# A first modulation quarter in two halves, and nine projection groups begun over three channel quarters

## The chip, the cores and the metric

The kernel runs on one core of a Trainium2 chip. The metric is the device time of one execution in microseconds (us); lower is better. Three runs of the kernel before took 2329.36 to 2330.72 us, median 2330.3.

## What is computed

Two streams of 128 tokens with 2048 channels (context and latent) go through two layers. Each layer begins like this, and the rest follows from the column blocks of one wide projection:

```python
def trunk_layer(x, mod, l, p, lower_bounds, hg_s0, s5_s0_re, s5_s0_im, ctx_k, ctx_v, rope):
    bsz, seq, _ = x.shape
    shift, scale, gate = jnp.split(mod, 3, axis=-1)
    h = rms_norm(x, p['norm_w'][l]) * (1 + scale[:, None, :]) + shift[:, None, :]
    (hg_q, hg_i, hg_ff, hg_fb, hg_g, at_q, at_k, at_v, at_g,
     s5_u, s5_g, merge_raw) = split_columns(h @ p['w_in'][l])
```

`mod` is `silu(c) @ w_mod[l] + b_mod[l]`, one vector of 3 x 2048 per stream. The blocks feed an HGRN2 recurrence, grouped-query attention and an S5 state-space scan; the three results are merged by gates, projected (w_out), gated and added to x.

## The kernel before, in words

**Layout.** Both streams are worked on together. h lies transposed, channels on partitions: 16 k-tiles of 128 channels. A channel quarter is four k-tiles (512 channels). h is kept as a rounded part (hh) and a rest (hl), each in a tile of tag H8 for two quarters; H8 has four buffers.

**Projections.** `gemm` (line 160) takes w_in in pieces of 512 KB (two k-tiles by 512 columns), three buffers of them. ScalarE rounds a k-tile of weights (wh, line 138), VectorE subtracts (wl, line 139), and TensorE adds three products for each stream: 12 matmuls of 512 columns a piece (lines 178 to 180). wh and wl have four buffers each. `in_group` does this for one group of 512 columns, named u 0, aq 0, aq 1, akv 0, q 0, ff 0, fb 0, i 0, u 1 and so on (`GROUPS`).

**Modulation.** `mod_part` (line 245) makes one quarter of shift and scale (512 channels of each) from eight weight tiles of 1 MB; each tile is 16 matmuls of 256 columns with 32 columns of c as stationary operand, four column strips side by side (line 274). A bias transfer on POOL, an add, two transposes, two copies and one more operation end it. `normed` (line 311) then scales x (xn), transposes it and applies shift and scale: stream 0 on VectorE (line 328), stream 1 on ScalarE (line 330), then splits into hh and hl.

**The opening of layer 0.** `build` issues c and x (two transfers of 1 MB) on ACT's queue; `square` and `token_rstd` make the norm's factor. Part 0 of the modulation runs first, with buffers that are free so early (`PTAGS`). In `layer`, nine groups (the first eight of `GROUPS` and q 1) are then begun: their sums over quarter 0 are copied from PSUM to their places by ScalarE (`begin`, line 344), and their sums over quarter 1 are added there by VectorE (line 342). Meanwhile a side generator issues modulation parts 1 to 3; `side_work` takes `SRATE` = 0.67 of a weight tile from it for every piece. After that quarters 2 and 3 of h are made, and `group` (line 365) completes each begun group with eight k-tiles and one more add.

**What follows.** u 0 goes to `s5_half`, whose `s5_quarter` (line 785) prepares a quarter in the tiles Bl, S16 (Sb), CC and scans it in 64 steps of four VectorE operations (lines 828 to 834). There are four such quarters in a layer, one after another, since these tiles have one buffer each. aq and akv go to attention, q, ff, fb, i to the HGRN2 units (`hgrn_unit`), each level of which waits for the one before. `s5_finish` (line 1034) splits the S5 result into ghl and multiplies it by w_glu.

**Order of the work.** The program's order on each engine and queue is planned ahead of the run by a priority per instruction: `with self.prio(base)` gives base plus a running number, and of what is ready the lowest number goes first. P_MIX is 0, P_SCAN 500,000, P_LAST 900,000, P_TOP 1,000,000 (weights, their splitting, evacuation), P_CHAIN 2,000,000, P_S5 3,000,000, P_PREP 5,000,000 and P_PE (projection matmuls) 6,000,000. On the chip each engine runs its list in that order. Weight transfers go through SP's queue.

The functions with the lines of the profile:

Of the kernel before, what the change touches and what calls it, by code (L numbers as in the profile page):

```python
# [20 lines left out]
D = 2048  # L21
T = 128
L = 2
# [3 lines left out]
NP = T // 2  # L27
RAW = 3
MB = 2
PTAGS = [(t, 2) for t in ("Bl", "S16", "ys")] + [(("k4", "k4"), 1)] + [("H8", 2)] * 4  # L30
STAGS = (("H8", 2),)
HF = ((1, 1, 1, 1), (0, 0, 0, 0))
SRATE = 0.67
MTAGS = ((("k4", "q4"), 1), (("k4", "q4"), 1), (("k4", "k4"), 1))
MRATE = (0.36, 0.13)
MAGIC = 1.5 * 2.0 ** 23
# [25 lines left out]
class Builder:  # L62
    def __init__(self, tc, ctx, io):
        self.tc, self.nc, self.io = tc, tc.nc, io
        self.seq = 0
        pool = lambda name, bufs, **kw: ctx.enter_context(tc.tile_pool(name=name, bufs=bufs, **kw))
        self.cp = pool("const", 1)
        self.wp = pool("weights", 4)
        self.sb = pool("sb", 1)
        self.bufs = dict(H8=4, Z8=2, Bl=1, CC=1, S16=1, uT=1, U2=1, ys=1, q4=2, kv=2,  # L70
                         mo=1, st=10, k2=6, k4=3, gt=4, sm=18, s5i=4, p=4, sb=1, sc=1, s5t=1)
        self.pg = pool("pg", 4, space=PSUM)
        self.pm = pool("pm", 2, space=PSUM)
        self.pb = pool("pb", 2, space=PSUM)
        self.dr = pool("scratch", 1, space=DRAM)
        self.uid = 0
# [122 lines left out]

    def condition(self):  # L200
        nc = self.nc
        c = self.const("c", (128, 80))[:, 0:32]
        nc.scalar.dma_start(c, self.io["cT"])
        self.cT = self.const("cs", (128, 64))
        nc.gpsimd.memset(self.cT, 0.0)
        sg = self.t2("sg", (128, 32))
        nc.scalar.activation(sg, c, AF.Sigmoid)
        nc.vector.tensor_mul(self.cT[:, 0:32], c, sg)
# [36 lines left out]
    def mod_part(self, l, part, prio, tags, plan):  # L245
# [3 lines left out]

        nc, io = self.nc, self.io  # L250
        with self.prio(prio):
            bm = self.t("mo", "bm", (128, 352))[:, 0:256]
            src = io["b_mod"][l, part]
            nc.gpsimd.dma_start(bm, bass.AP(src.tensor, src.offset, [[256, 4], [0, 32], [1, 256]]))
        kb = 0
# [41 lines left out]
                self.mods[part] = mt  # L297
        yield True


    def square(self, ssq, x, s, n):
        junk = self.tg("junk")
# [2 lines left out]
    def token_rstd(self, ssq):  # L305
        tot = self.ts("tot", (128, 2))
        self.nc.vector.tensor_reduce(tot, ssq, AX.X, ALU.add)
        r = self.rstd(tot, 2, D)
        return [r[:, s:s + 1] for s in range(2)]

    def normed(self, x, rs, q):

# [28 lines left out]
        with self.prio(P_TOP):  # L341
            self.nc.vector.tensor_add(dst, dst, ps)

    def begin(self, l, name, idx, q):

        ps = self.in_group(l, name, idx, 4 * q, 4 * q + 4)
        if q == 0:
            self.begun[name, idx] = self.places(name, idx)
        for dst, p in zip(self.begun[name, idx], ps):
            if q == 0:  # L350
                self.evac(p, dst)
            else:
                self.add(dst, p)
# [11 lines left out]
    def group(self, l, name, idx, func=None):  # L365
        dst = self.begun.pop((name, idx), None)
        if dst is None:
            ps = self.in_group(l, name, idx)
            dst = self.places(name, idx)
            for s in range(2):  # L370
                self.evac(ps[s], dst[s], func)
            return dst
        ps = self.in_group(l, name, idx, 8, 16)
        for s in range(2):
            self.add(dst[s], ps[s])
            if func is not None:
                with self.prio(P_TOP):
                    self.nc.scalar.activation(dst[s], dst[s], func)
        return dst
# [262 lines left out]
    def s5_params(self, l):  # L642
# [3 lines left out]
        nc, io = self.nc, self.io  # L646
        tt, ts = nc.vector.tensor_tensor, nc.vector.tensor_scalar
        par = self.t2("par", (128, 3, 64))
        nc.scalar.dma_start(par, io["s5_par"][l])
        ar, ai, ld = (par[:, i] for i in range(3))  # L650
        wks, cnt = [], [0]

# [206 lines left out]

    def layer(self, l, x, rs):  # L860
        nc, io = self.nc, self.io
        with self.prio(P_CHAIN):
            self.normed(x, rs, 0)
        if l == 0:
            def parts():
                for p in range(1, 4):
                    yield from self.mod_part(0, p, P_CHAIN, itertools.cycle(STAGS), [("b", 8, 1)])

            self.start_side(parts(), SRATE)
            for q in range(2):  # L870
                if q == 1:
                    while 1 not in self.mods:
                        next(self.side)
                    with self.prio(P_CHAIN):
                        self.normed(x, rs, 1)
                for name, idx in GROUPS[:8] + [("q", 1)]:
                    self.begin(l, name, idx, q)
            self.finish_side()
        with self.prio(P_CHAIN):
            for q in range(2 if l == 0 else 1, 4):  # L880
                self.normed(x, rs, q)
        with self.prio(P_PREP):
            bc = lambda src: bass.AP(src.tensor, src.offset + l * 128, [[0, 128], [1, 128]])
# [188 lines left out]
    def build(self):  # L1072
        nc, io = self.nc, self.io
        self.side = None
        self.s5p, self.s5sc, self.begun, self.mods = {}, {}, {}, {}
        with self.prio(P_CHAIN):
            self.condition()
            x = [self.t8("x") for _ in range(2)]
            for s in range(2):
                nc.scalar.dma_start(x[s], io["x"][s])  # L1080
            self.ident = self.const("ident", (128, 128), src=io["ident"])
            self.normw = self.const("normw", (128, L, 16), src=io["norm_w"])
        with self.prio(P_LAST):
            ssq = self.ts("ssq", (128, 2, 4))
            for s in range(2):
                for n in range(4):
                    self.square(ssq, x, s, n)
            rs = self.token_rstd(ssq)
        for _ in self.mod_part(0, 0, P_CHAIN, iter(PTAGS), [("g", 8, 1)]):
            pass  # L1090
        with self.prio(P_PREP):
            self.setup()
            for l in range(L):
                self.s5_params(l)
        for l in range(L):
            x, rs = self.layer(l, x, rs)
            if l + 1 < L:
                def gates():
                    tags = itertools.cycle(MTAGS)
                    for p in (4, 5):  # L1100
                        yield from self.mod_part(L - 1, p, P_PE, tags, [("m", MB, MB)] * (8 // MB))

                self.gates = gates()
        with self.prio(P_TOP):
            self.final(x, rs)
# [9 lines left out]
def _mod_parts(w):  # L1115

    h = D // 4
    return np.concatenate([w[..., o + q * h:o + q * h + h] for q in range(4) for o in (0, D)] + [w[..., 2 * D:]], axis=-1)


def _layouts(a):
# [4 lines left out]
    out["norm_w"] = ca(a["norm_w"].reshape(L, 16, 128).transpose(2, 0, 1))  # L1126
    out["w_mod"] = ca(_mod_parts(a["w_mod"]).reshape(L, 8, 2, 128, 6, 1024).transpose(0, 4, 1, 3, 2, 5).reshape(L, 6, 8, 128, 2048))
    out["b_mod"] = _mod_parts(a["b_mod"]).reshape(L, 6, 1024)
    w_in = np.empty((L, len(GROUPS), 8, 128, 1024), np.float32)
    for l in range(L):  # L1130
        for gi, (n, h) in enumerate(GROUPS):
# [77 lines left out]
```

## Time and profile before

| | us |
|---|---|
| median of three runs | 2330.3 |
| the profiled execution | 2331.88 |
| its span, first to last instruction | 2330.1 |
| TensorE busy | 2257.9 |
| VectorE busy | 1798.2 |
| ScalarE busy | 1180.8 |

The span lies within the profiled execution, whose time also holds 1.8 us around it. Busy time of TensorE (PE) holds overlap of pipelined matmuls. DVE is VectorE, ACT ScalarE, POOL GpSimd, SP the queue engine; a q behind a name means its instruction queue, and PEld is the loading of stationary operands. A row of the timeline gives start, length, engine, line, operation, output<-input, shapes and count, and in brackets the idle time before it with what ended it.

### The profile page before, as it was taken

The page shows a single profiled execution, that of the slowest core. Times are in us where ns is not written, and L with a number is a line of the kernel's source. Part 1 is how long each engine was busy: PE and PEld are TensorE (multiplying, and loading weights), DVE is VectorE, ACT ScalarE, POOL GpSimd, SP SyncE. Part 2 cuts the span into 40 slices and gives each one's busy share as a digit, 9 for nine tenths or more (in the row PEclk, how much of TensorE's full clock was granted, in tenths as well). Part 3 has the DMA queues.
Part 4 walks back from the last instruction along what each step waited for, and adds up shares of the span by engine and source line. Part 5 has one row for each costly group of instructions (what it writes and reads, how often), then busy time and mean ns, then how long its engine had stood idle before and what let it go on. Part 6 is the DMA issues. An engine that isn't in the chain of part 4 may idle for free.

```text
span 2330.1 us, 38207 instructions
## 1 busy us (share of the span) xinstructions
PE 2257.9 (97%) x13192; PEld 1812.2 (78%) x13192; DVE 1798.2 (77%) x4835; ACT 1180.8 (51%) x2061; POOL 133.9 (6%) x244
## 2 busy tenths in 40 slices
PE   4999999999999999999998999999999999999997
PEld 2777877888887776887777888888878877887886
DVE  5856899799879868865565798899959968956555
ACT  3536645555554343544446565555564544454454
POOL 2000000100000100000010001000010010000000
PEclk9999999999999999999999999999999999999999
DMA  8994554355557878677874554454545677656765
GB/s 313 342 341 142 165 172 137 110 162 184 178 165 258 295 267 298 220 251 265 305 231 138 163 174 153 132 160 155 188 155 190 194 245 240 198 179 219 240 202 181
DMA packets 131490, 483.85 MB, mean 208 GB/s; under 512 B 17200, under 2 KB 17808, under 8 KB 126944
## 3 DMA queue, kind: packets, MB, share of 16 engines
q1 hardware_dynamic: 120528, 454.09, 58.2%
q0 software_dynamic: 9472, 23.97, 3.3%
q10 hardware_dynamic: 1296, 3.36, 0.4%
q8 instruction: 103, 1.69, 0.3%
q14 instruction: 91, 0.75, 0.1%
HBM read 474.36 MB, written 6.98 MB: 207 GB/s over the span
## 4 chain that ended last, share of the span: by engine, by line
PE 82%; DVE 8%; DMA 7%; issue 2%; ACT 1%; SPq 0%; POOL 0%; DVEq 0%; ACTq 0%; POOLq 0%
PE g L178 23%; PE g L180 23%; PE g L179 22%; DMA raw<-w_in 3%; DVE wl L139 3%; PE mod L274 3%; PE bu L816 3%; PE lv L432 2%; DMA raw<-w_br 2%; DMA wm<-w_mod 2%; PE tr L134 2%; PE yp L847 1%; DVE p L830 1%; DVE Sb L834 1%; ACT wh L138 1%
## 5 line engine op out<-in xcount | busy, mean ns | idle before, releaser
L138 ACT CAST wh<-raw 128x512 fp32r<-128x512 f32 x1344 | 819.4, 622 | 925.0 <-PE g L179 459.8
L139 DVE TENSOR_TENSOR wl<-raw,wh 128x512 fp32r<-128x512 f32 x1344 | 915.5, 689 | 368.5 <-ACT wh L138 319.1
L178 PE MATMUL g<-wh,hl 128*128 128x512 f32 x1984 | 785.1, 396 | 6.4 <-ACT wh L138 2.7
L179 PE MATMUL g<-wh,hh 128*128 128x512 f32 x1984 | 777.9, 392 | 0.0
L180 PE MATMUL g<-wl,hh 128*128 128x512 f32 x1984 | 700.9, 398 | 0.4 <-DVE wl L139 0.3
L178 PEld LDWEIGHTS g<-wh,hl 128*128 128x128 f32 x1984 | 373.5, 188 | 99.4 <-ACT wh L138 8.2
L179 PEld LDWEIGHTS g<-wh,hh 128*128 128x128 f32 x1984 | 373.6, 188 | 75.7 <-issue 0.2
L180 PEld LDWEIGHTS g<-wl,hh 128*128 128x128 f32 x1984 | 366.6, 189 | 82.5 <-DVE wl L139 5.8
L178 PE MATMUL g<-wh,ol 128*128 128x512 f32 x384 | 152.0, 396 | 2.5 <-ACT wh L138 2.3
L828 DVE TENSOR_TENSOR p<-s5sc,Sb 128x64 f32<-128x64 f32 x512 | 140.8, 275 | 14.9 <-ACT Sb L820 5.9
L179 PE MATMUL g<-wh,oh 128*128 128x512 f32 x384 | 149.9, 390 | 0.0
L834 DVE TENSOR_TENSOR Sb<-Sb,p 128x64 f32<-128x64 f32 x512 | 141.7, 277 | 8.9
L830 DVE TENSOR_TENSOR p<-s5sc,Sb 128x64 f32<-128x64 f32 x512 | 139.2, 272 | 0.0
L180 PE MATMUL g<-wl,oh 128*128 128x512 f32 x384 | 132.0, 393 | 0.8 <-DVE wl L139 0.8
L274 PE MATMUL mod<-wm,cs 128*32 128x256 f32 x1536 | 104.5, 404 | 26.6 <-DMA wm<-w_mod 20.1
L833 DVE TENSOR_TENSOR p<-p,p 128x64 f32<-128x64 f32 x512 | 113.6, 222 | 6.1
L274 PEld LDWEIGHTS mod<-wm,cs 128*32 128x32 f32 x1536 | 44.7, 113 | 77.1 <-DMA wm<-w_mod 24.1
L179 PE MATMUL g<-wh,mt 128*128 128x512 f32 x256 | 99.8, 390 | 0.0
L178 PE MATMUL g<-wh,mt 128*128 128x512 f32 x256 | 99.7, 389 | 0.0
L178 PEld LDWEIGHTS g<-wh,ol 128*128 128x128 f32 x384 | 72.1, 188 | 20.3 <-ACT wh L138 4.6
L180 PEld LDWEIGHTS g<-wl,oh 128*128 128x128 f32 x384 | 71.5, 188 | 17.6 <-DVE wl L139 2.4
L180 PE MATMUL g<-wl,mt 128*128 128x512 f32 x256 | 83.5, 393 | 1.7 <-DVE wl L139 1.7
(315 smaller groups left out, 2116.8 us busy)
## 6 DMA issues: line engine op xcount, KB each, us to landing
raw<-w_in SPq DMA_DIRECT2D x496, 512.0 KB, 3.8
wm<-w_mod SPq DMA_DIRECT2D x130, 512.0 KB, 7.2
raw<-w_br SPq DMA_DIRECT2D x96, 512.0 KB, 4.2
raw<-w_out SPq DMA_DIRECT2D x64, 512.0 KB, 4.3
wm<-w_mod SPq DMA_DIRECT2D x31, 1024.0 KB, 7.4
raw<-w_glu SPq DMA_DIRECT2D x16, 512.0 KB, 3.9
gb<-gate_d POOLq DMA_DIRECT2D x16, 256.0 KB, 6.0
x<-x ACTq DMA_DIRECT2D x2, 1024.0 KB, 14.0
```

Of the source, the lines that this page charges most:

```text
L134: nc.tensor.transpose(ps[:, k], src[:, k * 128:(k + 1) * 128], self.ident)
L138: self.nc.scalar.copy(hi, src)
L139: self.nc.vector.tensor_sub(lo, src, hi.bitcast(F32))
L178: nc.tensor.matmul(ps[s], lo(k)[:, sl], wh, start=(k == 0), stop=False)
L179: nc.tensor.matmul(ps[s], hi(k)[:, sl], wh, start=False, stop=False)
L180: nc.tensor.matmul(ps[s], hi(k)[:, sl], wl, start=False, stop=(k == nk - 1))
L274: nc.tensor.matmul(ps[32 * i:32 * i + 32, 0:256], self.cT[:, 2 * k:2 * k + 32], ws[k - 2 * k0][:, i * 256:i * 256 + 256], start=(k0 == kb ...
L816: nc.tensor.matmul(pps[x][:, j2, k], Bl[pr, d, ri, k, j2, :], U2[pr, j2, 2 * qh + k].rearrange("p s t -> p (s t)"), start=True, stop=True, ...
L828: tt(p0.rearrange("p d (j s) -> p d j s", s=2), view(sc, qd * 32, [[16, 2], [1, 16], [0, 2]]), view(Sb, i, [[ds, 2], [2 * W, 16], [W, 2]]) ...
L830: tt(p1, view(sc, 128 + qd * 64, [[32, 2], [16, 2], [1, 16]]), view(Sb, i + RI, [[ds, 2], [-RI, 2], [W, 16]]), ALU.mult)
L833: tt(p0, p0, p1, ALU.add)
L834: tt(cur, cur, p0, ALU.add)
```

## The change

The first modulation quarter of layer 0 (part 0) is computed in two halves of 256 channels, each from four tiles of 1 MB in a new layout (32 matmuls of 128 columns a tile); `mod_half(0)` stands before the layer, `mod_half(1)` is the first work of the side generator. x is issued on SP's queue instead of ACT's, at the same priority. `first_turned` transposes the first quarter of x times the factor before the modulation is there and leaves it in PSUM (both buffers of bank b); `normed_half` applies a half to it. The nine groups are begun in four steps, over k-tiles 0 to 2, 2 to 4, 4 to 8 and 8 to 12, each step with its own rate of side work, and `group` completes them with the last four k-tiles. The S5 parameters, computed in `build` before, are issued within the side work, their two transfers on SP at P_TOP. Part 3 of the modulation takes its buffers from Bl, S16 and ys. Two tiles lose padding and the small tag gets two more buffers.

```diff
-PTAGS = [(t, 2) for t in ("Bl", "S16", "ys")] + [(("k4", "k4"), 1)] + [("H8", 2)] * 4
-STAGS = (("H8", 2),)
+HTAGS = (("Bl", "S16", "ys", "H8"), ("H8", "H8", "Bl", "S16"))
+STAGS = (None, (("H8", 2),), (("H8", 2),), (("Bl", 2), ("S16", 2), ("ys", 2)))
-SRATE = 0.67
+SRATE = (0.45, 0.8, 0.5, 0.5)
...
-                         mo=1, st=10, k2=6, k4=3, gt=4, sm=18, s5i=4, p=4, sb=1, sc=1, s5t=1)
+                         mo=1, st=10, k2=6, k4=3, gt=4, sm=20, s5i=4, p=4, sb=1, sc=1, s5t=1)
...
-        c = self.const("c", (128, 80))[:, 0:32]
+        c = self.const("c", (128, 64))[:, 0:32]
...
-            bm = self.t("mo", "bm", (128, 352))[:, 0:256]
+            bm = self.t("mo", "bm", (128, 256))
...
+    def mod_half(self, h):
+        nc, io = self.nc, self.io
+        with self.prio(P_CHAIN):
+            bm = self.t("mo", "bm", (128, 256))[:, 0:128]
+            src = io["b_mod0"][h]
+            nc.gpsimd.dma_start(bm, bass.AP(src.tensor, src.offset, [[128, 4], [0, 32], [1, 128]]))
+            ps = self.pg.tile([128, 512], F32, tag="g", name=self.nm("mod"))
+        for i4, tag in enumerate(HTAGS[h]):
+            with self.prio(P_TOP):
+                w = self.t(tag, "wm", (128, 2048))
+                nc.sync.dma_start(w, io["w_mod0"][h, i4])
+            with self.prio(P_CHAIN):
+                for c in range(4):
+                    k = 4 * i4 + c
+                    for i in range(4):
+                        nc.tensor.matmul(ps[32 * i:32 * i + 32, 0:128], self.cT[:, 2 * k:2 * k + 32],
+                                         w[:, c * 512 + i * 128:c * 512 + i * 128 + 128], start=(k == 0),
+                                         stop=(k == 15), tile_position=(0, 32 * i))
+            if i4 < 3:
+                yield True
+        with self.prio(P_LAST):
+            nc.vector.tensor_add(bm, bm, ps[:, 0:128])
+            tr = self.transpose4(bm, 1)
+            mt = self.cp.tile([128, 2, 2, 2], F32, tag=f"modH{h}", name=self.nm("modT"))
+            nc.vector.tensor_copy(view(mt, 0, [[4, 2], [2, 2], [1, 2]]), view(tr, 0, [[64, 2], [1, 2], [32, 2]]))
+            nc.vector.scalar_tensor_tensor(mt[:, 1], mt[:, 1], 1.0, view(self.normw, 2 * h, [[0, 2], [1, 2]]),
+                                           ALU.add, ALU.mult)
+            self.halves[h] = mt
+        yield True
...
+    def first_turned(self, x, rs):
+        self.turned = []
+        for s in range(2):
+            xn = self.tg("xn")
+            self.nc.vector.tensor_scalar(xn, x[s][:, 0:512], rs[s], None, ALU.mult)
+            self.turned.append(self.transpose4(xn, ps=self.psb("tr")))
+        self.hh = [self.t("H8", "hh", (128, 8, 256), F32R)]
+        self.hl = [self.t("H8", "hl", (128, 8, 256), F32R)]
+
+    def normed_half(self, h):
...
+            hf = self.tg("hf", (128, 2, 128))
+            for j in range(2):
+                scale, shift, ps = mt[:, 1, s, j:j + 1], mt[:, 0, s, j:j + 1], self.turned[s][:, 2 * h + j]
...
+            sl = (slice(None), slice(2 * h, 2 * h + 2), slice(s * 128, s * 128 + 128))
+            self.split_from(hf, self.hh[0][sl], self.hl[0][sl])
...
-        ps = self.in_group(l, name, idx, 8, 16)
+        ps = self.in_group(l, name, idx, 12, 16)
...
-        nc.scalar.dma_start(par, io["s5_par"][l])
+        with self.prio(P_TOP):
+            nc.sync.dma_start(par, io["s5_par"][l])
...
             def parts():
+                yield from self.mod_half(1)
                 for p in range(1, 4):
-                    yield from self.mod_part(0, p, P_CHAIN, itertools.cycle(STAGS), [("b", 8, 1)])
...
+                    if p < 3:
+                        with self.prio(P_PREP):
+                            self.s5_params(p - 1)
+                    yield from self.mod_part(0, p, P_CHAIN, itertools.cycle(STAGS[p]), [("b", 8, 1)])
+
+            with self.prio(P_LAST):
+                self.normed_half(0)
+            self.start_side(parts(), 0)
+            for i, (k0, k1) in enumerate(((0, 2), (2, 4), (4, 8), (8, 12))):
+                if i == 1:
+                    while 1 not in self.halves:
+                        next(self.side)
+                    with self.prio(P_LAST):
+                        self.normed_half(1)
+                self.side_rate = SRATE[i]
+                if i > 1:
+                    while i - 1 not in self.mods:
                         next(self.side)
                     with self.prio(P_CHAIN):
-                        self.normed(x, rs, 1)
+                        self.normed(x, rs, i - 1)
                 for name, idx in GROUPS[:8] + [("q", 1)]:
-                    self.begin(l, name, idx, q)
+                    self.begin(l, name, idx, k0, k1)
             self.finish_side()
...
             for s in range(2):
-                nc.scalar.dma_start(x[s], io["x"][s])
+                nc.sync.dma_start(x[s], io["x"][s])
...
-        for _ in self.mod_part(0, 0, P_CHAIN, iter(PTAGS), [("g", 8, 1)]):
+            self.first_turned(x, rs)
+        for _ in self.mod_half(0):
             pass
         with self.prio(P_PREP):
             self.setup()
-            for l in range(L):
-                self.s5_params(l)
```

## Rows read from the trace of the kernel before

**Rows 1.** The page: the chain that ended last, share of the span by engine.

```profile
PE 82%; DVE 8%; DMA 7%; issue 2%; ACT 1%; SPq 0%; POOL 0%; DVEq 0%; ACTq 0%; POOLq 0%
```

**Rows 2.** Windows of 20 us: length, busy us of each engine, clock, DMA share, GB/s.

```profile
0.00:20.00 20.00, 5.24 (x48) 1.79 (x48) 0.19 (x1) 2.52 (x5) 7.75 (x19) 1.00 0.92 345
...
60.00:80.00 20.00, 20.00 (x132) 13.79 (x131) 18.05 (x99) 9.38 (x17) 0.00 (x0) 1.00 0.94 350
```

**Rows 3.** Timeline of the opening, all engines: start, us, engine, line, operation.

```profile
0.74 18.38 SPq L265 DMA_DIRECT2D wm<-w_mod  x9
1.18 0.94 ACTq L1080 DMA_DIRECT2D x<-x  x2
...
3.20 0.55 POOL L793 DMA_DIRECT2D C<-s_c  x1
...
5.27 0.53 POOL L121 DMA_DIRECT2D eye<-eye  x1
...
18.99 0.63 ACT L303 ACTIVATE junk<-x 128x512 f32<-128x512 f32 x1 [12.91 <-DMA wm<-w_mod]
...
26.54 0.49 DVE L322 TENSOR_SCALAR xn<-x,r 128x512 f32<-128x512 f32 x1
...
36.00 1.86 PE L274 MATMUL mod<-wm,cs 128*32 128x256 f32 x16 [0.50 <-DMA wm<-w_mod]
...
44.29 1.38 DVE L328 TENSOR_SCALAR hf<-tr,modT 128x128 f32<-128x128 f32 x4
```

**Rows 4.** Timeline of PE, 46 to 64 us, where the gemms begin.

```profile
47.62 0.79 PE L178 MATMUL g<-wh,hl 128*128 128x512 f32 x1 [0.32 <-DVE hl L139]
...
51.72 0.40 PE L179 MATMUL g<-wh,hh 128*128 128x512 f32 x1
51.95 0.40 PE L180 MATMUL g<-wl,hh 128*128 128x512 f32 x1
52.28 1.07 PE L274 MATMUL mod<-wm,cs 128*32 128x256 f32 x16
53.28 0.50 PE L178 MATMUL g<-wh,hl 128*128 128x512 f32 x1
```

**Rows 5.** A window of 2 us: PE's granted clock is the figure behind POOL.

```profile
42.00:44.00 2.00, 0.00 (x0) 0.00 (x0) 2.00 (x14) 0.00 (x0) 0.00 (x0) 0.50 0.72 259
```

**Rows 6.** Timeline of PE about the end of the second quarter.

```profile
176.93 0.39 PE L180 MATMUL g<-wl,hh 128*128 128x512 f32 x1
177.91 1.07 PE L274 MATMUL mod<-wm,cs 128*32 128x256 f32 x16 [0.60 <-DMA wm<-w_mod]
...
183.24 0.50 PE L178 MATMUL g<-wh,hl 128*128 128x512 f32 x1 [0.26 <-DVE hl L139]
```

**Rows 7.** Groups by line, 47 to 178 us.

```profile
L139 DVE TENSOR_TENSOR wl<-raw,wh 128x512 fp32r<-128x512 f32 x72 | 49.4, 692 | 30.0 <-ACT wh L138 21.7 <-PE g L180 4.5 <-PE g L179 3.8
```

**Rows 8.** Timeline of VectorE: the last add of u 0, the first scan step.

```profile
196.55 0.68 DVE L342 TENSOR_TENSOR u<-u,g 128x512 f32<-128x512 f32 x1
...
239.94 0.27 DVE L828 TENSOR_TENSOR p<-s5sc,Sb 128x64 f32<-128x64 f32 x1 [2.10 <-ACT Sb L820]
```

**Rows 9.** Line 834, the scan's last operation: length of stretch, busy us (count).

```profile
240.00:394.00 154.00, 17.71 (x64) 1.00 0.52 163
394.00:462.00 68.00, 0.00 (x0) 1.00 0.34 106
...
626.00:677.00 51.00, 0.00 (x0) 1.00 0.44 139
...
850.00:964.00 114.00, 17.70 (x64) 1.00 0.84 287
```

**Rows 10.** VectorE and PE where layer 0's S5 result enters its gemm.

```profile
977.07 0.68 DVE L139 TENSOR_TENSOR ghl<-ys,ghl 128x512 fp32r<-128x512 f32 x1
...
992.34 0.39 PE L178 MATMUL g<-wh,ghl 128*128 128x512 f32 x1
```

**Rows 11.** Timeline of PE, 383 to 394 us.

```profile
390.43 0.50 PE L178 MATMUL g<-wh,hl 128*128 128x512 f32 x1 [1.50 <-ACT ff L386]
```

More of the change, by code (lines that the diff above doesn't have):

```diff
@@ L309, in token_rstd @@
         return [r[:, s:s + 1] for s in range(2)]
+    def first_turned(self, x, rs):
[7 more added lines that the diff above has]
+    def normed_half(self, h):
+        nc = self.nc
+        mt = self.halves[h]
+        for s in range(2):
+            hf = self.tg("hf", (128, 2, 128))
+            for j in range(2):
+                scale, shift, ps = mt[:, 1, s, j:j + 1], mt[:, 0, s, j:j + 1], self.turned[s][:, 2 * h + j]
+                if HF[s][j]:
+                    nc.vector.tensor_scalar(hf[:, j], ps, scale, shift, ALU.mult, ALU.add)
+                else:
+                    nc.scalar.activation(hf[:, j], ps, AF.Identity, scale=scale, bias=shift)
+            sl = (slice(None), slice(2 * h, 2 * h + 2), slice(s * 128, s * 128 + 128))
+            self.split_from(hf, self.hh[0][sl], self.hl[0][sl])
     def normed(self, x, rs, q):
@@ L342, in add, with begin @@
             self.nc.vector.tensor_add(dst, dst, ps)
-    def begin(self, l, name, idx, q):
-        ps = self.in_group(l, name, idx, 4 * q, 4 * q + 4)
-        if q == 0:
+    def begin(self, l, name, idx, k0, k1):
+        ps = self.in_group(l, name, idx, k0, k1)
+        if k0 == 0:
             self.begun[name, idx] = self.places(name, idx)
         for dst, p in zip(self.begun[name, idx], ps):
-            if q == 0:
+            if k0 == 0:
                 self.evac(p, dst)
@@ L861, in layer @@
         nc, io = self.nc, self.io
-        with self.prio(P_CHAIN):
-            self.normed(x, rs, 0)
         if l == 0:
             def parts():
+                yield from self.mod_half(1)
                 for p in range(1, 4):
-                    yield from self.mod_part(0, p, P_CHAIN, itertools.cycle(STAGS), [("b", 8, 1)])
[L869 to L872, printed above, removed]
+                    if p < 3:
[14 more added lines that the diff above has]
+                    while i - 1 not in self.mods:
                         next(self.side)
                     with self.prio(P_CHAIN):
-                        self.normed(x, rs, 1)
+                        self.normed(x, rs, i - 1)
                 for name, idx in GROUPS[:8] + [("q", 1)]:
-                    self.begin(l, name, idx, q)
+                    self.begin(l, name, idx, k0, k1)
             self.finish_side()
         with self.prio(P_CHAIN):
-            for q in range(2 if l == 0 else 1, 4):
+            for q in range(3 if l == 0 else 0, 4):
                 self.normed(x, rs, q)
@@ L1074, in build @@
         self.side = None
-        self.s5p, self.s5sc, self.begun, self.mods = {}, {}, {}, {}
+        self.s5p, self.s5sc, self.begun, self.mods, self.halves = {}, {}, {}, {}, {}
         with self.prio(P_CHAIN):
@@ L1128, in _layouts @@
     out["b_mod"] = _mod_parts(a["b_mod"]).reshape(L, 6, 1024)
+    cols = [np.r_[256 * h:256 * h + 256, D + 256 * h:D + 256 * h + 256] for h in range(2)]
+    out["w_mod0"] = np.stack([a["w_mod"][0][:, c].reshape(4, 4, 128, 512).transpose(0, 2, 1, 3).reshape(4, 128, 2048)
+                              for c in cols])
+    out["b_mod0"] = np.stack([a["b_mod"][0][c] for c in cols])
     w_in = np.empty((L, len(GROUPS), 8, 128, 1024), np.float32)
```

## Prediction

> **What bounds the kernel now.** The chain that ended last is read first: 82% of it is TensorE [rows 1]. So time is to be had where TensorE stands idle, and the windows show where: in the first 20 us it is busy for 5.24, from 60 us on for all of a window [rows 2]. In the opening the DMA share is 0.92 at 345 GB/s: weights of the first modulation quarter are awaited. The timeline gives the steps [rows 3]: SP issues nine transfers for that quarter, ACT the two of x, the last modulation matmuls start at 36.00, the modulated h is made from 44.29, and the first projection matmul starts at 47.62 [rows 4]. A second hole comes after the second quarter: the last matmul starts at 176.93 and lasts 0.23, the next projection starts at 183.24 [rows 6], 6.1 us later, because the last modulation tile arrives last. Beside TensorE runs a second chain, the S5 scan on VectorE. Its first step is at 239.94, after u 0 was complete at 196.55 + 0.68 [rows 8]; four quarters of 64 steps follow each other [rows 9], and the result meets TensorE at 992.34 [rows 10].
>
> **The change part by part.** The sum is made against the profiled execution, 2331.88 us (span 2330.1 and 1.8 around it); the median of the runs is 1.6 lower.
>
> *Start of the projections.* Ahead of the first matmul now stand 4 MB of modulation weights for 8. What decides is x. It leaves ACT's queue, where its two issues were free beside SP's nine [rows 3], and joins SP's. Transfers with a lower priority number are issued first: on POOL, C (P_S5, 3 million) went out at 3.20 ahead of eye (P_PREP, 5 million) at 5.27, although the code calls for eye first [rows 3]. x keeps P_CHAIN, 2 million; weights and w_in pieces have P_TOP, 1 million. So I put x behind what is free to go: the half's four tiles (4 MB), three w_in pieces in their three buffers (1.5 MB), the first tile of the second half in the spare H8 buffer (1 MB) and the two par transfers (0.2 MB), which also moved to this queue. Before, 8 MB of weights and 2 MB of x had come by 36.00: 3.6 us per MB, small loads included. With x itself that makes 8.7 MB, 31.3 us. Then four squares of 0.63 (2.5); from squares to xn it took 26.54 - 18.99 = 7.55 for eight, so 2.5 besides the squares; xn 0.49, its transposes 0.6 (an estimate, about three matmuls of 0.23); half of the 1.38 of hf (0.7); half of the 1.95 from the end of hf (45.67) to 47.62 (1.0) [rows 3, 4]; 1 for hops between engines. Sum 40.1, **gain 7.5**. The half itself is ready by then.
>
> The Trainium skill, "DMA: Bandwidth & Descriptors", Queues, rings and completion order, says that each DMA engine takes turns between the queues but consumes one ring's descriptors in order. The rows agree in that x landed in time for squares at 18.99 amid nine weight tiles. By that rule a move from ACT's ring to SP's takes x's share away unless x is issued first.
>
> *Second half.* Its four tiles hold 32 matmuls of 128 columns each, where a tile of before holds 16 of 256 columns. Sixteen of those cost 1.00 between projections (52.28 to 53.28) [rows 4] and 1.86 in the opening [rows 3]. Bounds per tile: 1.0 if columns count, 2.0 if instructions do, 3.7 at the opening's pace; I take 1.5, since the interleaved row is the nearest. Two of the four tiles should pass before 40 us while TensorE waits anyway, so two lie in its way: **loss 3.0**. Were that cover gone, 6.
>
> The Trainium skill, "TensorEngine Tiling (Array Packing)", Key Properties, says that changing the tiling mode drains TensorE, which speaks against slipping more 32-column work between projections. Rows agree in kind: the matmul ahead of the group holds 0.33 instead of 0.23 (51.95 to 52.28), already near the 1.00 that I use. Four more visits at 0.2 would be 0.8 by that rule, inside my bounds.
>
> *A third quarter begun early.* It moves 18 pieces of 12 matmuls forward; at 0.23 each (51.72 to 51.95 [rows 4]) a piece is 2.7 us and 18 are 49, the same work as before, later. What it buys is that modulation parts 1 to 3 (24 MB) spread over 54 pieces (27 MB) instead of 36, so TensorE, not DMA, ends the stage, and the last part is ready four pieces ahead. Of the hole of 6.1 [rows 6] the modulation tile's 1.0 and about 0.5 of transposes stay: **gain 4.6**. The rate of the second step (0.8 in nine pieces) leaves part 1's eighth tile to the boundary; its chain is between the 4.5 worked out under the rivals and the 9.8 from 37.86 to 47.62 [rows 3, 4], and up to four halves of pieces already cast (5.4) lie in front of it: **loss 1.0**, from 0 to 4.
>
> *VectorE and PSUM.* 36 more adds of 0.68 [rows 8] are 24.5 us. In the first stage VectorE was busy 18.05 of 20 [rows 2], but part of that is S5 parameter work of lowest priority. In the nine-piece step two subtractions of 0.69 [rows 7] and two adds make 2.7 us per piece, beside TensorE's 2.7 plus 0.8 tiles of modulation: it fits, so 0, with up to 5 if it doesn't. The transposes of both streams hold both buffers of bank b until the second half is applied; part 1's accumulation waits behind that, and SP's later H8 tiles behind part 1. This costs nothing while projections feed TensorE; else it is the 1.0 above. On SP a tile of the second half waits until matmuls release its buffer, with w_in pieces queued behind it; up to 40 us nothing consumes pieces, so 0 there, and inside the 1.0 later. The bias transfer is one more POOL issue, off the path.
>
> *S5.* Parameters are computed later in VectorE's gaps: 0; were the gaps missing, their lowest priority makes them wait until the first scan needs them. Part 3 now sits in Bl and S16, so the first scan's preparation waits for its end. Padding: no instruction; 0, unsigned.
>
> Clock: where TensorE had waited, the granted clock was 0.50, the 1.2 GHz level [rows 5], and the first matmuls of before ran at it. It will again; no difference.
>
> Sum: 7.5 - 3.0 + 4.6 - 1.0 = 8.1. 2331.9 - 8.1 - 1.6 = **2322 us**. Own range 2316 to 2330, by 4 us of x's landing and the bounds above. About 0.2%, 4.7 us, is what a measurement of this kernel can tell from no change.
>
> **Rivals.**
> *x goes first.* If x is issued ahead of the weights, only 6 MB (21.6 us) precede the half's last matmuls (to 24.5); add, transpose, copies, hf and split without parameter work between them take 4.5 by the same rows: first projection at 29. Gain 18.6, all four tiles now in the way (-6), DMA tighter at the boundaries (-2), +4.6: 15.2, so **2315**. For it: both x transfers stand first in the code. Against: POOL's order.
>
> *S5 takes over (slower).* Projections from 40, the 129.5 us that two quarters took (47.62 to 177.16), 49 for the third, 4 as above: 222.6; u 0's last two pieces end at 228, and the 43.4 us from its add to the scan [rows 8] make 271.4, **31.5 us later** than 239.94. Slack: the last split of the S5 result ends at 977.75 and TensorE takes it at 992.34 [rows 10], 14.6; between the first scans lie 68 us, between the next 51 [rows 9], 17. Together 31.6: past a start of 271 the scan sets the layer's end. If Bl and S16 come free late and preparation (about 9 us, estimated) is not hidden, it starts at 280: **2339**. Against: the first scan took 154 us, the last 114 [rows 9], since attention shares VectorE; a later start shares less of it.
>
> *Handed back.* At 390.43 TensorE waited 1.50 for ScalarE to empty ff's PSUM [rows 11], which waits for the HGRN levels. If these do not come earlier, what was won earlier ends here: **2330**.
>
> **How the numbers follow.** Forecast 0.45 (0.38 beyond 0.2%, 0.07 within), x first 0.32, handed back 0.10, S5 slower 0.13. Faster 0.70, same 0.17, slower 0.13. The range reaches from the rival x first with its tiles at column pace (2311) to the beginning of the slower case (2334).
>
> **What would show it.** x's squares at 26 to 34 us and the first projection near 40 (right), below 32 (x first); the hole at the quarter's end under 2 us; per-tile cost of the half 1 to 2 us; first scan step 260 to 272 and the S5 gemm before 988. Wrong: a first projection after 45, a scan past 275, or TensorE idle for over 6 us more between 340 and 460.

## The result and the profile after

The changed kernel takes 2353.1 us (median of four runs, 2345.3 to 2354.8) against 2330.5: ratio 1.0091, 95% interval 1.0068 to 1.0113, so **slower by 0.9%**. Run again beside the experiments it took 2351.5, ratio 1.0090 (1.0077 to 1.0103). The profiled execution is the fastest of its four runs: 2345.29, span 2343.4. The two profiles so differ by 13.3 us in span; the medians differ by 19 to 23.

The page's chain, share of the span by engine, which answers to [rows 1]:

```profile
PE 87%; DVE 4%; DMA 3%; ACT 1%; issue 1%; SPq 0%; DVEq 0%; ACTq 0%
```

It shows less waiting for DMA and VectorE than before, on a longer span; it doesn't tell where the loss is. The opening answers to [rows 3]; timeline of all engines:

```profile
0.74 2.16 SPq L311 DMA_DIRECT2D wm<-w_mod  x4
...
2.94 1.54 SPq L168 DMA_DIRECT2D raw<-w_in  x3
...
6.12 0.86 SPq L1147 DMA_DIRECT2D x<-x  x2
...
9.29 3.71 SPq L311 DMA_DIRECT2D wm<-w_mod  x2
...
26.48 0.63 ACT L334 ACTIVATE junk<-x 128x512 f32<-128x512 f32 x1 [3.63 <-DMA x<-x]
...
29.59 0.63 ACT L334 ACTIVATE junk<-x 128x512 f32<-128x512 f32 x1 [0.55 <-DMA x<-x]
...
38.06 0.80 PE L178 MATMUL g<-wh,hl 128*128 128x512 f32 x1 [0.86 <-DVE hl L139]
```

x goes out behind the four tiles and three pieces and ahead of the second half's first tiles, its squares begin 7.5 us later than before, and the first projection still starts 9.6 us earlier than 47.62 [rows 4]. The second half between projections, timeline of PE:

```profile
45.74 0.39 PE L180 MATMUL g<-wl,hh 128*128 128x512 f32 x1
46.06 1.08 PE L316 MATMUL mod<-wm,cs 128*32 128x128 f32 x32
47.07 0.50 PE L178 MATMUL g<-wh,hl 128*128 128x512 f32 x1
...
51.38 2.83 PE L316 MATMUL mod<-wm,cs 128*32 128x128 f32 x96
54.13 0.50 PE L178 MATMUL g<-wh,hl 128*128 128x512 f32 x1
```

A tile of 32 matmuls takes 1.01 from start to next start, three take 2.75: as long as tiles of 16 matmuls with twice the columns. All four tiles of the second half stand here, behind the first projection. Further on, timeline of PE where TensorE stands still:

```profile
110.42 0.66 PE L134 MATMUL tr<-ident,xn 128*128 128x128 f32 x4
114.09 1.38 PE L274 MATMUL mod<-wm,cs 128*32 128x256 f32 x16 [3.01 <-DMA wm<-w_mod]
...
142.20 1.07 PE L274 MATMUL mod<-wm,cs 128*32 128x256 f32 x16
144.64 0.72 PE L180 MATMUL g<-wl,hh 128*128 128x512 f32 x2 [1.37 <-DVE wl L139]
...
149.33 0.73 PE L180 MATMUL g<-wl,hh 128*128 128x512 f32 x2 [1.66 <-DVE wl L139]
```

and VectorE at the last two of them:

```profile
143.90 1.28 DVE L139 TENSOR_TENSOR wl<-raw,wh 128x512 fp32r<-128x512 f32 x2
145.11 3.45 DVE L786 TENSOR_TENSOR Sb<-Sb 64x256 f32<-64x256 f32 x8
148.59 1.90 DVE L139 TENSOR_TENSOR wl<-raw,wh 128x512 fp32r<-128x512 f32 x3
```

Preparation of the S5 tiles (Sb) runs ahead of the weights' rest wl there; in the kernel before it ran between 60 and 84 us. Afterwards the hole of [rows 6] is gone; windows (PE busy first; the last three figures are clock, DMA share, GB/s):

```profile
100.00:120.00 20.00, 16.99 (x148) 11.13 (x142) 17.57 (x94) 5.76 (x12) 0.69 (x1) 0.91 0.97 375
180.00:200.00 20.00, 20.00 (x92) 16.54 (x91) 15.80 (x28) 11.60 (x21) 0.00 (x0) 1.00 0.56 187
```

In the second of them TensorE is full and the DMA share has fallen to 0.56: from here the third quarter runs at TensorE's pace. And then u 0 and the first scan step, timeline of VectorE, against [rows 8]:

```profile
238.66 1.28 DVE L398 TENSOR_TENSOR u<-u,g 128x512 f32<-128x512 f32 x2 [1.15 <-PE g L180]
...
288.26 0.28 DVE L885 TENSOR_TENSOR p<-s5sc,Sb 128x64 f32<-128x64 f32 x1 [0.66 <-ACT Sb L877]
```

The scan begins **48.3 us later** than before. Its stretches (line 891; length of stretch, busy us and count) against [rows 9]: the gaps between scans are shorter by 7 in the first case, longer by 3 in the second. The first scan is longer by 11, the second shorter by 20, the last by 4:

```profile
289.00:454.00 165.00, 17.46 (x64) 0.99 0.44 150
454.00:515.00 61.00, 0.26 (x1) 1.00 0.33 114
515.00:659.00 144.00, 17.43 (x64) 1.00 0.53 185
659.00:713.00 54.00, 0.28 (x1) 1.00 0.41 142
...
887.00:997.00 110.00, 17.56 (x64) 0.99 0.72 254
```

The second scan in the kernel before (line 834):

```profile
462.00:626.00 164.00, 17.61 (x64) 1.00 0.56 179
```

At the end of layer 0's scan, timeline of PE, against [rows 10]:

```profile
992.30 0.61 PE L180 MATMUL g<-wl,hh 128*128 128x512 f32 x2
997.16 1.08 PE L904 MATMUL yp<-Sb,C 128*32 128x128 f32 x16 [4.25 <-DVE Sb L891]
...
1004.19 0.62 PE L904 MATMUL yp<-Sb,C 128*32 128x128 f32 x16
1006.32 0.49 PE L178 MATMUL g<-wh,ghl 128*128 128x512 f32 x1 [1.51 <-DVE ghl L139]
```

TensorE has run out of projections, waits 4.25 for the scan's last step, does the S5 outputs while nothing else is left, and waits again for ghl. The same last yp matmuls in the kernel before:

```profile
969.91 0.62 PE L847 MATMUL yp<-Sb,C 128*32 128x128 f32 x16
```

There they started at 969.91 and the ghl gemm at 992.34 without a wait: 22.4 us of other work lay between, where 2.1 are the least that any run shows. **The scan, which had 20.3 us to spare at this place, now sets the layer's end.** The gemm is 14.0 late; the span is 13.3 longer.

How much TensorE stood idle, worked out from the starts of consecutive matmuls: each interval less the usual one of its form in the kernel before (0.227 for a projection matmul, 0.061 for a modulation matmul of 256 columns; half of that, 0.030, for one of 128). The time before the first matmul counts in the first row.

| stretch, us | before | after | difference |
|---|---|---|---|
| 0 to 50 | 40.1 | 35.8 | -4.3 |
| 50 to 100 | 2.6 | 3.0 | +0.4 |
| 100 to 150 | 2.2 | 9.9 | +7.7 |
| 150 to 225 | 8.1 | 0.9 | -7.2 |
| 225 to 300 | 2.3 | 5.2 | +2.9 |
| 300 to 975 | 45.3 | 48.2 | +2.9 |
| 975 to 1025 | 0.4 | 11.7 | +11.3 |

Up to 300 us the changed kernel is level with the one before (0.5 less idle). The loss is the last row, and some 3 us between. All rows together make 13.7, near the 13.3 between the two spans.

### The profile page after: what moved, and what is told of

Same layout as the page of the kernel before. It is cut to its first block, busy times and chain, and to the rows that moved or that the text cites. A ratio compares the mean times of both kernels' runs of the same rounds, so it can differ in the third digit from the quotient of the medians.

```text
span 2343.4 us, 38492 instructions
## 1 busy us (share of the span) xinstructions
PE 2257.8 (96%) x13320; PEld 1820.1 (78%) x13320; DVE 1822.2 (78%) x4875; ACT 1182.8 (50%) x2064; POOL 144.1 (6%) x245
## 4 chain that ended last, share of the span: by engine, by line
PE 87%; DVE 4%; DMA 3%; ACT 1%; issue 1%; SPq 0%; DVEq 0%; ACTq 0%
PE g L178 24%; PE g L180 24%; PE g L179 24%; PE mod L274 3%; PE bu L873 2%; PE lv L488 2%; PE tr L134 2%; PE yp L904 1%; DVE wl L139 1%; DMA wm<-w_mod 1%; DMA raw<-w_in 1%; DMA raw<-w_br 1%; PE yp L897 1%; PE sc L612 0%; DVE Sb L786 0%
## 5 line engine op out<-in xcount | busy, mean ns | idle before, releaser
L180 PE MATMUL g<-wl,hh 128*128 128x512 f32 x1984 | 690.5, 398 | 5.7 <-DVE wl L139 5.7
L274 PE MATMUL mod<-wm,cs 128*32 128x256 f32 x1408 | 88.1, 384 | 7.5 <-DMA wm<-w_mod 7.5
L178 PEld LDWEIGHTS g<-wh,ol 128*128 128x128 f32 x384 | 72.1, 188 | 17.8 <-ACT wh L138 2.0
L180 PEld LDWEIGHTS g<-wl,oh 128*128 128x128 f32 x384 | 71.4, 188 | 17.4 <-DVE wl L139 2.2
L179 PEld LDWEIGHTS g<-wh,oh 128*128 128x128 f32 x384 | 72.1, 188 | 15.2 <-issue 0.8
```

The lines of the kernel that those rows point to most:

```text
L178: nc.tensor.matmul(ps[s], lo(k)[:, sl], wh, start=(k == 0), stop=False)
L179: nc.tensor.matmul(ps[s], hi(k)[:, sl], wh, start=False, stop=False)
L180: nc.tensor.matmul(ps[s], hi(k)[:, sl], wl, start=False, stop=(k == nk - 1))
L274: nc.tensor.matmul(ps[32 * i:32 * i + 32, 0:256], self.cT[:, 2 * k:2 * k + 32], ws[k - 2 * k0][:, i * 256:i * 256 + 256], start=(k0 == kb ...
```

## The experiments

The theory S: the late S5 chain is the loss. Its rivals put the loss ahead of the scan: on the place of x (X, in e1), on the opening (O, in e2 to e4), and later on TensorE's own work at large, halves, added sums and boundaries (W). Ratios are against runs of the kernel before on the same chip, whose medians were 2331.4 to 2332.6 beside the experiments; e9 to e12 ran on another chip than e1 to e8; the times of events are those of the profiled executions, in us. "yp" is the start of the last yp matmuls of layer 0, "wait" TensorE's idle time just ahead of the ghl gemm.

| kernel | median, us | ratio (95%) | first projection | first scan step | yp | ghl gemm | wait |
|---|---|---|---|---|---|---|---|
| before | 2330.5 | | 47.62 | 239.94 | 969.91 | 992.34 | 0 |
| after, again | 2351.5 | 1.0090 (1.0077 to 1.0103) | 38.21 | 289.20 | 1007.57 | 1009.70 | 1.51 |
| e1 x first | 2345.4 | 1.0055 (1.0038 to 1.0072) | 30.78 | 278.75 | 999.21 | 1001.33 | 1.51 |
| e2 two quarters | 2340.1 | 1.0036 (1.0022 to 1.0050) | 38.65 | 244.92 | 975.05 | 997.48 | 0 |
| e3 after, short scan | 2341.6 | 1.0039 (1.0026 to 1.0052) | 38.85 | 288.72 | 958.43 | 997.18 | 0 |
| e4 before, short scan | 2327.9 | 0.9976 (0.9964 to 0.9987) | 46.73 | 239.51 | 926.97 | 988.78 | 0 |
| e5 third quarter for 4 | 2334.3 | 1.0009 (0.9995 to 1.0022) | 37.91 | 260.45 | 983.79 | 991.26 | 0 |
| e6 before, u late | 2333.8 | 1.0013 (1.0001 to 1.0026) | 46.99 | 283.28 | 995.36 | 997.49 | 1.51 |
| e7 before, padding | 2332.2 | 1.0001 (0.9991 to 1.0012) | 46.67 | 238.73 | 968.16 | 990.59 | 0 |
| e8 x first, third for u 0 | 2328.0 | 0.9981 (0.9967 to 0.9996) | 30.93 | 229.26 | 962.93 | 985.36 | 0 |
| e9 third for u 0 | 2335.2 | 1.0014 (1.0001 to 1.0026) | 38.69 | 240.30 | 967.36 | 989.78 | 0 |
| e10 x first, short scan | 2332.6 | 1.0011 (0.9997 to 1.0025) | 31.46 | 282.86 | 953.49 | 992.24 | 0 |
| e12 x first, no third | 2327.5 | 0.9989 (0.9974 to 1.0003) | 31.96 | 233.73 | 962.64 | 985.07 | 0 |

**e1, x ahead of everything.**

```diff
             for s in range(2):
-                nc.sync.dma_start(x[s], io["x"][s])
+                with self.prio(P_TOP):
+                    nc.sync.dma_start(x[s], io["x"][s])
```

> The changed kernel with x issued ahead of the first half's weights on SP's queue. Theory S (the S5 scan chain of layer 0 starts late, because u 0 is complete only after the third quarter and the last modulation part, and its end sets the layer's end): the first projection comes at about 29 us, but what ends the opening is the traffic up to the last modulation part, so the first scan step moves by less than 10 us (from 289 to 280 to 289) and the time is 2338 to 2352. Theory X (the loss is x, late in the queue): 2330 or less.

S held. TensorE stands idle 9.5 us less than in the changed kernel up to 300 (45.3 against 54.8), yet the ghl gemm starts only 5.0 earlier, because the scan is only 9.5 earlier and is still what it waits for. It also shows what the prediction's first rival would have given for the first projection: 30.8, not 29, and slower than before all the same.

**e2, no third quarter ahead.**

```diff
-SRATE = (0.45, 0.8, 0.5, 0.5)
+SRATE = (0.45, 0.8, 0.9)
...
-            for i, (k0, k1) in enumerate(((0, 2), (2, 4), (4, 8), (8, 12))):
+            for i, (k0, k1) in enumerate(((0, 2), (2, 4), (4, 8))):
```

(`group` completes from k-tile 8 again; part 3 loads into H8.)

> The changed kernel with the third quarter not begun early (nine groups over k-tiles 0 to 8, completed with eight; part 3 of the modulation back in H8 and issued with part 2 at 0.9 tiles a piece); halves and x as in the change. Theory S: u 0 is complete near 200 us, the first scan step comes at 240 to 250 and the time is 2320 to 2333, no slower than before. Theory O (the halves, the queue order or the padding lose the time in the opening itself): 2342 or more.

Both missed: 2340, between them. The scan starts 5.0 late, far inside its margin, and the gemm doesn't wait. The opening gave its head start back; timeline of PE:

```profile
105.87 1.07 PE L274 MATMUL mod<-wm,cs 128*32 128x256 f32 x16
108.59 1.07 PE L274 MATMUL mod<-wm,cs 128*32 128x256 f32 x16 [1.66 <-DMA wm<-w_mod]
114.32 1.93 PE L274 MATMUL mod<-wm,cs 128*32 128x256 f32 x16 [4.65 <-DMA wm<-w_mod]
...
180.35 1.07 PE L274 MATMUL mod<-wm,cs 128*32 128x256 f32 x16
...
185.74 0.63 PE L134 MATMUL tr<-ident,xn 128*128 128x128 f32 x4 [2.89 <-DVE modT L295]
```

TensorE meets the same transfers earlier and waits for them: DMA was busy all through this stage before (0.94 in [rows 2], 0.87 to 0.98 in windows of 20 us from 80 to 180), and the last modulation matmuls start at 180.35 where they started at 177.91 [rows 6], the chain behind them still standing open for 2.89. So the first projection 9 us earlier was worth nothing by itself.

**e3 and e4, a shorter first scan, in the changed kernel and in the one before.** 32 of the 64 steps of layer 0's first scan are left out in both.

```diff
-            for i in range(NP):
+            for i in range(NP // 2 if (l, qd) == (0, 0) else NP):
```

> The changed kernel; the first S5 quarter of layer 0 is scanned over 32 of its 64 steps (the second half of that scan is left out). Theory S: some 75 us are taken out of the chain that sets the layer's end, TensorE no longer waits near 992 us, and the time falls by 12 to 22 us, to 2326 to 2335. Theory O: the scan has slack, so the time falls by less than 6 us.

> The kernel before with the same omission (32 of 64 steps of the first scan of layer 0). Under both theories the chain had slack here: 2324 to 2331, a fall of less than 6 us. A fall of 10 us or more would say that the scan chain sets the time of the kernel before too.

e4 as expected: the scan wasn't what bound the kernel before. In e3 the gemm no longer waits, starts 9.1 earlier, and the time falls by 10 to 11.5: that much of the loss went with the scan. It lies at the join: by the measure of the idle table e3 stands idle for some 51 us from 300 to 975, no less than the changed kernel's 48, and for 0.3 from 975 to 1025. But the time misses S's range and doesn't fall to e4's: 13.7 us are left between the two, so S alone was not all of it. Of these, 8.4 are there at the ghl gemm, and the stage from 300 to 975 holds them: e4 is idle there for some 43, e3 for 51.

**e6, the S5 chain late in the kernel before.**

```diff
-        u_half(0)
+        if l > 0:
+            u_half(0)
...
         kv = self.group(l, "akv", 0)
+        if l == 0:
+            u_half(0)
```

> The kernel before with one thing moved: the last eight channels of the first u group run behind aq 0, aq 1 and akv instead of ahead of them, in layer 0 alone; nothing is added. Three groups of 10.9 us move ahead of u, so u 0 should be complete near 230 and the first S5 scan start near 273 instead of 240.7. Theory S (the late start of the S5 chain is what the change loses on top of its opening): 8 to 18 us above the kernel before, 2340 to 2350. Theory W (the halves, the added sums and the boundaries on TensorE are the loss, and the S5 chain has some 30 us to spare): at most 3 us, 2330 to 2335.

By the numbers W won: a scan that starts 43.3 later (10 more than expected) costs 2.5 us in the median. The trace says why, timeline of VectorE's first scan step and of PE:

```profile
283.28 0.28 DVE L828 TENSOR_TENSOR p<-s5sc,Sb 128x64 f32<-128x64 f32 x1 [1.11 <-ACT Sb L820]
```

```profile
995.36 0.62 PE L847 MATMUL yp<-Sb,C 128*32 128x128 f32 x16
997.49 0.50 PE L178 MATMUL g<-wh,ghl 128*128 128x512 f32 x1 [1.51 <-DVE ghl L139]
```

Of 43.3, 17.8 are gone by the last yp (25.5 late) and 20.3 lie ahead of the gemm; 5.2 come through. Lateness is free up to some 34 to 38 us; beyond it, it comes through at the gemm, 5.2 late here with a span 6.4 longer, while the median's 2.5 (0.2 to 6 by its interval) can't tell how much of it the time shows. The theory had to become: the changed kernel overruns this margin. There 48.3 less 14.0 absorbed by the last yp is 34.3, and less the 20.3 ahead of the gemm 14.0, what the gemm is late. The split is read from that same trace; that such a margin exists is what e6 shows by itself.

**e5, the third quarter for four groups; e9, for u 0 alone; e8, u 0 alone and x first.**

```diff
-                for name, idx in GROUPS[:8] + [("q", 1)]:
+                for name, idx in (GROUPS[:8] + [("q", 1)])[:4 if i == 3 else 9]:
```

(4 in e5, with 1.0 tiles a piece in the last step; 1 in e8 and e9, with 2.0. `group` completes the other groups from k-tile 8.)

> The changed kernel, in which only four groups (u 0, aq 0, aq 1, akv) are begun over the third channel quarter; the other five do it together with the fourth, as in the kernel before. Five groups of 5.44 us go behind u's last quarter: u 0 complete near 212 instead of 239, first scan near 258 instead of 289.6. S: with about half of the delay gone, 2338 to 2346. W (the work of the halves and the boundaries stays, only ten of the added sums go): 2347 or more, within 5 us of the changed kernel.

> The changed kernel with the third channel quarter begun early for u 0 alone; x stays where the change put it. S (the S5 chain ends layer 0 in the changed kernel, TensorE's own loss is the smaller part): u 0 complete near 195, first scan near 241, the scans' end near 965, so TensorE ends the layer: it lacks the 9 us that x first gives, glu near 1006, 2333 to 2340. W (TensorE's own loss is nearly all): 2344 or more, within 8 us of the changed kernel.

> The changed kernel with x loaded ahead of everything else on SyncE's queue and the third channel quarter begun early for u 0 alone. First projection near 31, u 0 complete between 185 and 197, first scan at 230 to 241, no later than before. S: the S5 chain starts on time and TensorE is ahead or level, so 2320 to 2333. A third reading, D (the stage is ended by the last modulation tile, which lands at 178 whatever comes ahead of it): TensorE stands where it did at u 0, 2331 to 2338, with holes of 5 us or more before 180. W: 2338 or more.

All three fell on S's side (e5 below its range). With the scan at 260 or earlier the gemm doesn't wait, and against the changed kernel e9 gives back 16.3 us. The pair e9 and e8 shows what x first is worth where the scan doesn't take it away: 7.2 us in the medians (6.4 when each is taken against the kernel before on its chip), 4.4 at the gemm.

**e7, the sizes of tiles alone, in the kernel before.**

```diff
-        c = self.const("c", (128, 80))[:, 0:32]
+        c = self.const("c", (128, 64))[:, 0:32]
...
-            bm = self.t("mo", "bm", (128, 352))[:, 0:256]
+            bm = self.t("mo", "bm", (128, 256))
```

(and twenty small tiles instead of eighteen)

> The kernel before with the changed kernel's buffer sizes alone: the condition tile 64 wide instead of 80, the bias tile 256 instead of 352, twenty small tiles instead of eighteen. No instruction is added or moved. S and W both expect no change, 2329 to 2335. A rival on where tiles lie in the on-chip memory expects 3 us or more.

No change, as both expected.

**e10, e1 with the short scan.** Edits of e1 and e3 together; the same 32 steps are left out.

> The variant with x ahead of everything on SyncE's queue and the third quarter begun for all nine groups, with 32 of the 64 steps of layer 0's first S5 scan left out (the S5 output of that quarter is then not the reference's). S: that variant was held back by the S5 chain alone, TensorE being ahead of the kernel before by some 5 us at 950; with 85 us less of scan TensorE ends the layer, glu near 1000, 2320 to 2333. W: the omission changes little, 2339 to 2346.

S held: 12.8 us less than e1 (12.3 when each is taken against the kernel before on its chip). The gemm follows the projections without a wait, timeline of PE:

```profile
991.78 0.62 PE L180 MATMUL g<-wl,hh 128*128 128x512 f32 x2
992.24 0.39 PE L178 MATMUL g<-wh,ghl 128*128 128x512 f32 x1
```

**e11, the changed kernel again.**

> The changed kernel as it is, on the chip and beside the runs of the others, so that it can be compared with them. S and W: 2343 to 2356, first scan near 290, last scan of layer 0 done near 997.

As expected (the last scan ends at 1000.1, 3 later than said); here the gemm starts 17.4 late and the span is 19.0 longer, so the larger loss of the medians goes the same way.

**e12, x first and no third quarter.** Edits of e1 and e2, with part 3 in Bl, S16 and ys.

> The changed kernel with x first and no third quarter begun early: nine groups over two quarters in three steps, the last two modulation parts both beside the third step at 0.9 tiles a piece, the last one in the Bl, S16 and ys buffers. S: the S5 chain starts on time (first scan at 230 to 245); what is missing beside the variant with u 0's third quarter is cover for the last modulation tiles, so 0 to 6 us above that one: 2328 to 2336. D (x first is worth nothing when no third quarter is there to fill the wait for the last tile): at the level of the variant with two quarters measured before, 2337 to 2342.

S held, and e2's two stalls were not the price of leaving the third quarter out: TensorE is idle for 5.2 from 100 to 125, where e2 has 9.1, and for 3.0 from 175 to 225, where e2 has 7.9. Which of the two edits did that, x or part 3's buffers, wasn't tried apart. With e8 it is the best version: 2327.5, 0.1% below the kernel before, an interval that just takes in no change; e8's doesn't. The gemm comes 7.3 before its time in [rows 10]:

```profile
984.61 0.62 PE L180 MATMUL g<-wl,hh 128*128 128x512 f32 x2
985.07 0.39 PE L178 MATMUL g<-wh,ghl 128*128 128x512 f32 x1
```

## Why the prediction was wrong

It said 2322 and faster; the case that came is its rival **S5 takes over**, which had 0.13.

*Where x goes* was right in kind: x went behind the four tiles and three pieces, and the first projection came at 38.06 for 40.1. The sum for x's landing was near by luck. It put 8.7 MB up to x's end at 3.6 us each, 31.3; the second half's first tile went out behind x, at 9.29, and par at 41.61, so only 7.5 MB were issued up to x. Its second transfer had landed by 29.59, 3.9 us per MB: the price was too low and the list too long. The Trainium skill, "DMA: Bandwidth & Descriptors", Queues, rings and completion order, has one ring's descriptors consumed in order; the trace agrees: x, issued at 6.12 behind seven transfers on SP's queue, was there for squares at 26.48 where ACT's queue had it at 18.99 [rows 3].

*Second half*: 1.0 per tile, the lower bound, for 1.5; but all four tiles lay in TensorE's way, not two, so it cost 3.8 for 3.0. Start and half together were to gain 7.5 - 3.0 = 4.5; the idle table has 4.3 up to 50 us and 3.9 up to 100. The Trainium skill, "TensorEngine Tiling (Array Packing)", Key Properties, has TensorE drained at a change of tiling mode; here the matmul ahead of the tile holds 0.32 for 0.23 (45.74 to 46.06), as in [rows 4], so ahead of a visit the effect stays at a tenth of a microsecond.

*Hole*: 4.6 forecast, 7.2 less idle between 150 and 225. Right in kind.

*Boundary and VectorE*: 1.0 and 0 forecast. From 100 to 125 TensorE was idle for 5.4 instead of 1.0, from 125 to 150 for 4.5 instead of 1.2: +4.4 at the boundary, a little past the bound of 4 (1.7 of the 5.4 are a lower clock, see the last section, where the forecast had "no difference" for the clock), and +3.3 where the S5 preparation stood ahead of wl, inside the bound of 5. The step "were the gaps missing, their lowest priority makes them wait" looked at priority numbers alone and at the parameters alone: what stood ahead of wl is the preparation that needs them, and though its number is higher (P_S5 against P_TOP), wl follows it in VectorE's list. Up to 225 the sum was 3.4 and not 8.1, and by 300 it was 0.5, with 2.9 lost from 225 on, and later 2.9 more. For the first 2.9 the trace shows but one wait, of 0.2, and they stay unexplained. In the later 2.9 stand 5.3 of waits for the softmax of attention, less what other waits there fell by; waits of PE from 240 to 460 in the changed kernel:

```profile
PE tr L134 <- ACT pr L618: 5.3, 2, 3.3
```

and in e9, where only u 0 had its third quarter early, the same 0.2 as in the kernel before:

```profile
PE tr L134 <- ACT pr L619: 0.2, 1, 0.2
```

They come with the third quarter for nine groups: 5.0 to 5.4 in e1, e3, e10 and e11, at most 0.2 in e2, e5, e8, e9 and e12. That the row maxima stand behind scan steps on VectorE there is argued, not tried.

**The step that failed** is the cost of the third quarter: "the same work as before, later", at 0 on TensorE, with the lateness of u 0 left to a rival whose margin it just met. The rival's mechanism came true, and its margin was right to a few us: it gave 14.6 at the join and 17 between the scans, 31.6 together; measured are 20.3 and 14.0, 34.3. That the two sums lie so near is luck. The 17 were read from gaps that would shrink, and the first gap gave 7 and the next took 3 back; what was absorbed came from the second scan, 20 shorter, against a first scan 11 longer. The rival's start was wrong: 271.4 forecast, 288.26 measured, past the 275 that the prediction named as a sign of being wrong. Two terms were mis-sized. u 0 was put at 228, with the two quarters at "the 129.5 us that two quarters took" from 40. Those 129.5 end ahead of the 24th modulation tile and its chain [rows 6] and hold no second half; with these and the stops above the third quarter began at 184, 146 us after the first projection, and u 0's last add started at 239.26, 11.3 late. From there to the scan it took 49.0 instead of 43.4, 5.6 more; it took 49.0 too in e1, e3, e10 and e11, where nine groups had their third quarter early, and 43.4 to 43.8 in e2, e8, e9 and e12. What fills these 5.6 wasn't tried. With a start of 288 the same working gives an overrun of 17 and the right sign. The forecast took a start 31.5 late against a margin of 31.6 as a tie, and gave the losing side 13%.

*Handed back* had next to nothing to hand back, 0.5 by 300 us; the wait for ff fell from 1.50 [rows 11] to 0.7. *x goes first* was excluded by the order of issues, and e1 shows that with the third quarter for nine groups it wouldn't have been faster. The range's lower end, 2311, doesn't follow from the working: four tiles at 1.0 in place of 1.5 take 2315 to 2313.

What stays open: of the 19 to 23 us, e3 and e10 show 10 to 13 as the scan's; e9 takes back 16, so some 3 to 6 belong to the third quarter without the scan, among them the softmax waits; the 3.1 that e9 itself lies above before is not explained, as its profiled execution has the ghl gemm 2.6 earlier. e4 gains 4.7 where the scan wasn't waited for, so a shorter scan relieves something else too (VectorE, as is argued); in e3's trace no such relief shows ahead of the join, but how much of e3's and e10's figures it is stays open.

## What to carry to other kernels

Work moved ahead on the bound engine moves something else back on it: look for whoever consumes the result that now comes last, and follow that consumer to the place where it meets the main engine again. Its margin is two numbers, the gap at the join, which the trace of the kernel before holds, and the shrinkage on the way, which that trace only hints at: a run that starts the second chain late and changes nothing else, as e6 does, measures both. Where lateness and margin come out equal, the error of the start decides, so it deserves the closest working. Don't put other groups' early work ahead of the group that heads the second chain: with the third quarter early for u 0 alone e9 is 16 us faster than the change, and e8, with x first as well, some 24. That beginning early for u 0 gains anything isn't shown: e12 does without it and is as fast.

## What was not expected

A standstill of 3 us inside the stage costs more than itself. Timeline of PE after the wait that ended at 114.09:

```profile
115.40 0.79 PE L178 MATMUL g<-wh,hl 128*128 128x512 f32 x1
115.99 0.63 PE L179 MATMUL g<-wh,hh 128*128 128x512 f32 x1
116.42 0.63 PE L180 MATMUL g<-wl,hh 128*128 128x512 f32 x1
...
118.36 0.40 PE L179 MATMUL g<-wh,hh 128*128 128x512 f32 x1
118.59 0.39 PE L180 MATMUL g<-wl,hh 128*128 128x512 f32 x1
```

The matmuls start 0.43 apart instead of 0.23 until 118, and the window from 100 to 120 has a granted clock of 0.91. Three windows of 1 us show where (PE busy first; the third figure from the end is the clock):

```profile
115.00:116.00 1.00, 1.00 (x10) 0.51 (x3) 1.00 (x10) 0.00 (x0) 0.00 (x0) 0.50 1.08 459
116.00:117.00 1.00, 1.00 (x4) 0.81 (x3) 1.00 (x10) 0.00 (x0) 0.00 (x0) 0.50 0.93 389
117.00:118.00 1.00, 1.00 (x4) 0.80 (x3) 0.27 (x3) 0.00 (x0) 0.00 (x0) 0.50 1.10 447
```

From 115 to 118 TensorE ran at the 1.2 GHz level, as where it had waited in the opening [rows 5]. The seven intervals from 115.40 to 118.36 take 2.96 instead of 1.61, the modulation tile ahead of them 1.31 instead of 1.01: 1.7 of the 5.4 us of idle from 100 to 125 are this.
